# Seven of eight query tiles on float16 parts, and weight readings queued behind the modulation transfers

## The chip, the cores and the metric

The kernel runs on one core of one Trainium2 chip. The metric is the device time of one execution in microseconds; the median of three runs is given, and one more execution was recorded by the hardware profiler. The engines are TensorE (PE, with PEld for its weight loads), VectorE (DVE), ScalarE (ACT), GpSimd (POOL) and SyncE (SP). SP and POOL issue most of the DMA transfers, each strictly in its own order. An instruction waits on its engine until its inputs are there and its output buffer is free, and everything behind it on that engine waits too.

## The reference

Two blocks of a diffusion transformer over 256 tokens `x` and 256 context tokens `ctx`, width 2048, all in float32. Layer 0 mixes by a Fourier transform, layer 1 is windowed attention with context keys. Each layer is modulated by a shift, a scale and a gate, which are products of `silu(c)` with `ada_w`.

```python
shift, scale, gate = split(silu(c) @ ada_w[i] + ada_b[i])      # the same for the context
h = rmsnorm(x, norm_g[i]) * (1 + scale) + shift
# layer 0
u, z = split(h @ fnet_w_in)                                    # 2048 -> 4096 + 4096
f = real(fft2(u by groups of 256)) ; f = f @ w_mix             # 16 groups
x = x + gate * ((f * silu(z)) @ w_out[0])                      # 4096 -> 2048
# layer 1
q, k, v, z = split(h @ attn_w_in)                              # q: 64 heads of 64, k and v: 8 heads
o = softmax(rope(q) rope(k)^T / 8 with window, context and sink) v
x = x + gate * ((o * silu(z)) @ w_out[1])
return rmsnorm(x, final_g)
```

## The kernel before, in words

The kernel keeps float32 accuracy by splitting each operand in a high and a low part and multiplying three times (`mm3`: high·high, high·low, low·high; lines L145 to L147). There are two kinds of parts. `half_split` makes float32r parts `wh`, `wl`: a cast on ScalarE (L66) and a subtraction on VectorE (L67). `split16` makes float16 parts in one tile `wf`: a scaled copy on ScalarE (L137) and a scaled subtraction on VectorE (L138). Float16 needs a scale per weight matrix, a power of two that is found from the sum of the squares of the whole matrix. So a weight that is to be split in float16 has to be read once ahead of time, which is called a reading here: POOL loads half a weight tile (512 KB of float32) as a bfloat16 tile `sn` of 256 KB (`scan_load`, L821), and ScalarE squares it and sums (`scan_sums`, L836).

The stages in order of time, with their approximate place in the span:

- 0 to 370 us: modulation of layer 0, Fourier part.
- 370 to 658 us, the z stage: 28 blocks `b` of 48 matmuls each (`ps<-act,wf`), each with one 1 MB weight tile `raw` (SP), `y` (256 KB, SP), and readings.
- 658 to 1003 us, the output projection of layer 0: 32 steps `i` of 48 matmuls (`ps<-y,wf`), two halves of the output (`sw`) of 16 steps (`kg`) each. A step has one `raw` tile of 1 MB, split in two halves `wf` (for `kg` 14 and 15 in float32r parts). The second half's first step needs a scale that is made on VectorE as the first half ends (L843 and around).
- 1003 to 1112 us: sums, keys and values of layer 1.
- 1112 to 1565 us: attention. Eight query tiles (`wq`), 32 z tiles and 32 attention blocks, interleaved: per query tile four z tiles and four blocks.
- to the end: output projection of layer 1.

Beside the z stage and the first projection run 64 modulation jobs (`ada_jobs`): each loads two 512 KB pieces of `ada_w`, `zr` on SP and `wa` on POOL, and VectorE multiplies and sums them with L792 (twice a piece, in the last third of the jobs once). A step of the projection takes one job, in steps 6 to 9 and 17 to 25 two, in steps 14 to 16 and from 28 on none (`ada_rate`). `cb` (1 MB) is loaded four times for the jobs. `wa` tiles lie in the pool `ws` (six buffers) together with the split weights; `sn` tiles in the pool `act` (33 buffers).

The order of instructions on each engine is set by a scheduler that runs the program on a model of the chip. `tc.issue_after(x)` gives it an order to keep on the engine of `x`: what is traced inside comes after `x` there. It makes no new wait between engines.

Layer 1 multiplies query tiles 0 to 3 from the float32r parts `hx1` (in the profile `ps<-wh,h` and `ps<-wl,h`) and tiles 4 to 7 from the float16 parts `hz` (`ps<-wf,hzx`). Their scale `upq` comes from 32 readings of the weights of tiles 4 to 7, all made in the z stage (`scan_loadsq`). In the projection, readings are made of the rest of `wo0` (`scan_loads`, steps 0 to 13) and of `wkv` and `wo1b` (`scan_loads1`, by `w_rate`: 1 or 2 in steps 10, 11, 14 to 18 and 20, 2 in step 22, 3 in steps 24 and 26 to 28).

Of the kernel before, what the change touches and what calls it, by code (L numbers as in the profile page):

```python
# [32 lines left out]
def tile_dit(ctx: ExitStack, tc: tile.TileContext, a: dict, out: bass.AP):  # L33
    nc = tc.nc
# [20 lines left out]
    def act(dt=F32):  # L55
        return actp.tile([P, 512], dt, tag="act", name="act")
# [12 lines left out]
    def half_split(t, i):  # L69
        h = wsp.tile([P, 1024], F32R, tag="ws", name="wh")  # L70
        l = wsp.tile([P, 1024], F32R, tag="ws", name="wl")
        split(h, l, t[:, i * 1024 : (i + 1) * 1024])
        return h, l
# [695 lines left out]
    def ada_jobs():  # L769
        for pieces in ((0,), (1, 2, 3)):  # L770
            for kh in range(2):
                cb = adap.tile([P, 2, 1024], F32, tag="cb", name="cb")
                with tc.issue_after(hs_end[2]):
                    nc.gpsimd.dma_start(cb, a["crow"][:, kh].broadcast_to([P, 2, 1024]))
                with tc.issue_after(hs_end[1]):
                    S.activation(cb, cb, AF.Silu)
                order = [(i, fg) for i in pieces for fg in range(8)]
                if kh == 1 and len(pieces) == 3:
                    thirds = [(3, fg) for fg in range(8)]
                    order = order[:4] + [o for pair in zip(order[4:12], thirds) for o in pair] + order[12:16]  # L780
                if True:
                    for i, fg in order:
                        for f in range(2):
                            q = slice(f * 1024, f * 1024 + 1024)
                            if f == 0:
                                wf = adat.tile([P, 1024], F32, tag="zr", name="zr", bufs=2)
                                nc.sync.dma_start(wf, a["adw"][i, kh, fg][:, q])
                            else:
                                wf = wsp.tile([P, 1024], F32, tag="ws", name="wa")
                                nc.gpsimd.dma_start(wf, a["adw"][i, kh, fg][:, q])  # L790
                            for s in range(2 if i < 3 else 1):
                                V.tensor_tensor_reduce(junk if s == 0 and i < 3 else wf, wf, cb[:, s], 1.0, 0.0, ALU.mult, ALU.add, acc[:, i, kh, fg * 2 + f, s : s + 1])  # L792
                        if kh == 1 and fg == 7:
                            ada_done(i)
                        yield
        while True:
            yield

    out0 = [False]
    ada = ada_jobs()  # L800


# [9 lines left out]
    yq = adab[:, 1, 0].rearrange("p k s -> p (k s)")  # L812
    wst = [a["wkv"][i] for i in range(8)] + [a["wo1b"][i] for i in range(12)] + [a["wo1c"][i] for i in range(6)]
    scans1 = iter(range(52))
    scansq = iter(range(32))
    qsn = c32.rearrange("p k c -> p (k c)")[:, 0:32]

    def scan_load(src, j, col):
        t = actp.tile([P, 1024], BF16, tag="act", name="sn")
        c = j % 2 * 1024  # L820
        nc.gpsimd.dma_start(t, src[:, c : c + 1024])  # L821
        pend.append((t, col))

    def scan_loadsq(n):
        for j in [next(scansq) for _ in range(n)]:
            scan_load(a["wq"][4 + j // 8, j // 2 % 4], j, qsn[:, j : j + 1])

    def scan_loads1(n):
        for j in [next(scans1) for _ in range(n)]:
            c = j + 64  # L830
            scan_load(wst[j // 2], j, scn[:, c : c + 1])
# [29 lines left out]
    with tc.tile_pool(name="yp", reuse_waits="tile", bufs=32) as ypool:  # L861
# [174 lines left out]
        for i in range(32):  # L1036
# [7 lines left out]
            if i < 14:  # L1044
                scan_loads({6: 1, 7: 1, 8: 1, 9: 1}.get(i, 2))
            scan_loads1(w_rate.get(i, 0))
            if i == 14:
                osc.append(half_scale(1, half_sum(1)))
            if kg == 14:
# [96 lines left out]
    with tc.tile_pool(name="h1", reuse_waits="tile", bufs=16) as h1p:  # L1146
# [136 lines left out]
        with tc.tile_pool(name="at", reuse_waits="tile", bufs=2) as at:  # L1283
# [88 lines left out]
            def finish_q(hk, oq):  # L1372
                sq = at.tile([P, 2, 4], F32, tag="sq", name="sq")
                for tb in range(2):
                    S.activation(act(), oq[tb], AF.Square, scale=dnq if hk >= 4 else 1.0, accum_out=sq[:, tb, 0:1])
                x, up, sc = (sq[:, :, c] for c in (1, 2, 3))
                qr = [act(), act()]
                tab = ropeq if hk >= 4 else rope
                roped(qr[0], oq[0], 0, actp, "act", tab=tab)
                V.tensor_scalar(x, sq[:, :, 0], 2.0**-70, None, op0=ALU.max)  # L1380
                V.tensor_scalar(x.bitcast(I32), x.bitcast(I32), 24, 23, op0=ALU.logical_shift_right, op1=ALU.logical_shift_left)
# [48 lines left out]
            def prep(u):  # L1430
                kind, n, i, _ = u
                if kind == "o":
                    return w1_next()
                src = (kind, n, i // 2)
                if src not in raws1:
                    raws1[src] = raw(a["wq"][n, i // 2] if kind == "q" else a["wz1"][n])
                return split16(raws1[src], i % 2, upq) if kind == "q" and n >= 4 else half_split(raws1[src], i % 2)

            ready = {}
            pe_last = [None]  # L1440
# [1 line left out]
            def emit_unit():  # L1442
# [17 lines left out]
                if kind == "q":  # L1460
# [5 lines left out]
                    for j in range(2):  # L1466
                        k = i * 2 + j
                        q = slice(j * 512, (j + 1) * 512)
                        for tb in range(2):
                            t = hz[k][0] if n >= 4 else hx1[k]  # L1470
                            pe_last[0] = mm3(o[tb], t[:, tb * P : (tb + 1) * P], t[:, N + tb * P : N + (tb + 1) * P], wh[:, q], wl[:, q], k == 0, k == KT - 1)
                    if i == 7:
                        finish_q(n, o)
# [367 lines left out]
```

## Time and profile before

| | us |
|---|---|
| median of three runs (lowest, highest) | 1754.69 (1754.27, 1757.89) |
| the profiled execution | 1755.04 |
| its span, first to last instruction | 1753.3 |
| TensorE busy in it | 1702.5 (97%) |
| VectorE busy | 1376.5 (79%) |
| ScalarE busy | 1125.1 (64%) |
| mean granted TensorE clock | 0.992 of full speed |

Busy time of matmuls overlaps itself, since they are pipelined: a float16 matmul of 512 columns is shown with 379 ns but a new one starts every 215 ns. So stalls of PE are read here from the number of matmuls in a stretch. In the table of transfers a reading is counted with the 256 KB that it writes, though it reads 512 KB.

### The profile page before, as it was taken

What the parts mean: (1) busy time and instruction counts of PE and PEld (TensorE: products, weight loads), DVE (VectorE), ACT (ScalarE), POOL (GpSimd) and SP (SyncE); (2) the same over time, 40 slices, a digit from 0 to 9 for tenths busy, and PEclk for the clock granted to TensorE, in tenths of its full rate; (3) what the DMA queues carried; (4) which work ended last, traced back from release to release, by engine and by line L of the source; (5) the groups of instructions that cost most, each with busy time, mean ns of one, the idle gap of its engine ahead of it and who ended that gap; (6) DMA issues with size and microseconds to landing.
All of it is one profiled execution on the core that took longest, in us unless ns stands there. A gap on an engine that the chain in (4) does not pass through costs nothing. (4 is left out here: it accounts for less than half of the span.)

```text
span 1753.3 us, 28081 instructions
## 1 busy us (share of the span) xinstructions
PE 1702.5 (97%) x10379; PEld 1095.3 (62%) x10379; DVE 1376.5 (79%) x2395; ACT 1125.1 (64%) x1997; POOL 248.2 (14%) x372
## 2 busy tenths in 40 slices
PE   6999999999999999799979999999999999999997
PEld 4679999644444444345434564678887667876464
DVE  5779889798676884785679578688999999987755
ACT  5545556477887875363414379668878878887643
POOL 0002111211211113101210112200000000051002
PEclk9999999999999999899989999999999999999999
DMA  9998999789998989786888569269989999988643
GB/s 394 418 355 253 275 271 264 294 254 301 305 307 259 321 280 255 255 305 218 241 273 308 168 240 354 91 191 257 232 224 233 240 252 245 214 225 298 224 169 120
DMA packets 252393, 455.04 MB, mean 260 GB/s; under 512 B 170480, under 2 KB 170880, under 8 KB 225376
## 3 DMA queue, kind: packets, MB, share of 16 engines
q1 hardware_dynamic: 197568, 335.60, 59.2%
q0 software_dynamic: 50544, 110.70, 24.9%
q10 hardware_dynamic: 4144, 6.95, 1.1%
q8 instruction: 81, 1.33, 0.3%
q14 instruction: 56, 0.46, 0.1%
HBM read 436.14 MB, written 12.59 MB: 256 GB/s over the span
## 5 line engine op out<-in xcount | busy, mean ns | idle before, releaser
L146 PE MATMUL ps<-act,wf 128*128 128x512 f16 x512 | 194.0, 379 | 0.0
L147 PE MATMUL ps<-act,wf 128*128 128x512 f16 x512 | 191.1, 379 | 0.0
L67 DVE TENSOR_TENSOR wl<-raw,wh 128x1024 fp32r<-128x1024 f32 x120 | 150.8, 1266 | 50.9 <-ACT wh L66 29.1
L145 PE MATMUL ps<-act,wf 128*128 128x512 f16 x512 | 189.8, 379 | 0.6 <-ACT wf L137 0.5
L145 PE MATMUL ps<-y,wf 128*128 128x512 f16 x448 | 172.6, 386 | 10.2 <-ACT wf L137 10.2
L147 PE MATMUL ps<-y,wf 128*128 128x512 f16 x448 | 170.3, 384 | 9.6 <-DVE wf L138 9.6
L146 PE MATMUL ps<-y,wf 128*128 128x512 f16 x448 | 172.9, 386 | 0.0
L147 PEld LDWEIGHTS <-wf 128*128 128x128 f16 x960 | 94.3, 98 | 125.3 <-DVE wf L138 11.0
L145 PEld LDWEIGHTS <-wf 128*128 128x128 f16 x960 | 94.3, 98 | 124.7 <-ACT wf L137 14.2
L146 PEld LDWEIGHTS <-wf 128*128 128x128 f16 x960 | 94.6, 98 | 111.1 <-issue 3.8
L66 ACT CAST wh<-raw 128x1024 fp32r<-128x1024 f32 x120 | 124.3, 1045 | 59.2 <-PE ps L146 33.5
L137 ACT ACTIVATE wf<-raw,nrm 128x1024 f16<-128x1024 f32 x56 | 62.9, 1142 | 130.4 <-DVE acc L792 103.3
L145 PE MATMUL ps<-h,wh 128*128 128x256 f32 x512 | 144.8, 283 | 0.0
L146 PE MATMUL ps<-h,wh 128*128 128x256 f32 x512 | 142.2, 278 | 0.0
L147 PE MATMUL ps<-h,wl 128*128 128x256 f32 x512 | 142.2, 278 | 0.0
L138 DVE SCALAR_TENSOR_TENSOR wf<-raw,adab,wf 128x1024 f16<-128x1024 f32 x82 | 112.2, 1380 | 30.3 <-ACT wf L137 30.2
L836 ACT ACTIVATE sn<-sn 128x1024 bf16<-128x1024 bf16 x121 | 126.3, 1044 | 11.7 <-DMA sn<-in_wq 6.9
L1520 ACT ACTIVATE p<-ps,mx 128x512 f32<-128x512 f32 x128 | 87.9, 687 | 61.3 <-DVE mx L1516 61.3
L137 ACT ACTIVATE wf<-raw,adab 128x1024 f16<-128x1024 f32 x82 | 91.9, 1142 | 40.4 <-PE ps L147 16.3
L138 DVE SCALAR_TENSOR_TENSOR wf<-raw,tn,wf 128x1024 f16<-128x1024 f32 x64 | 79.9, 1282 | 46.4 <-ACT wf L137 46.3
L145 PEld LDWEIGHTS ps<-h,wh 128*128 128x128 f32 x512 | 96.1, 188 | 7.4 <-issue 5.1
L792 DVE CUSTOM_DVE_ANT_0 junk<-wa,cb 128x1024 f32<-128x1024 f32 x48 | 58.6, 1221 | 51.2 <-DMA wa<-in_adw 51.0
(444 smaller groups left out, 4691.5 us busy)
## 6 DMA issues: line engine op xcount, KB each, us to landing
raw<-in_wz SPq DMA_DIRECT2D x64, 1024.0 KB, 6.9
raw<-in_awp SPq DMA_DIRECT2D x32, 1024.0 KB, 12.7
zr<-in_adw SPq DMA_DIRECT2D x64, 512.0 KB, 7.0
wa<-in_adw POOLq DMA_DIRECT2D x64, 512.0 KB, 6.8
raw<-in_wo SPq DMA_DIRECT2D x32, 1024.0 KB, 7.6
raw<-in_wq SPq DMA_DIRECT2D x32, 1024.0 KB, 5.7
raw<-in_wu SPq DMA_DIRECT2D x32, 1016.0 KB, 6.5
sn<-in_wo POOLq DMA_DIRECT2D x64, 256.0 KB, 9.9
```

The costliest lines, as they stand in the source:

```text
L66: last_cast[0] = S.copy(h, src).ins
L67: last_sub[0] = eng.tensor_tensor(l, src, h.bitcast(F32), op=ALU.subtract).ins
L137: last_cast[0] = S.activation(w[:, 0], src, AF.Copy, scale=up).ins
L138: last_sub[0] = V.scalar_tensor_tensor(w[:, 1], src, up, w[:, 0], op0=ALU.mult, op1=ALU.subtract).ins
L145: PE.matmul(o, wh, xh, start=start, stop=False)
L146: PE.matmul(o, wh, xl, start=False, stop=False)
L147: return PE.matmul(o, wl, xh, start=False, stop=stop).ins
L792: V.tensor_tensor_reduce(junk if s == 0 and i < 3 else wf, wf, cb[:, s], 1.0, 0.0, ALU.mult, ALU.add, acc[:, i, kh, fg * 2 + f, s : s + 1])
L836: S.activation(t, t, AF.Square, accum_out=c)
L1520: S.activation(pt[hh, tb], so[hh, tb], AF.Exp, bias=mx[:, hh, tb : tb + 1], scale=-1.0, accum_out=sm[:, hh, tb : tb + 1])
```

## The change

Three things are done together.

1. Query tiles 1 to 3 also use float16 parts: `n >= 4` and `hk >= 4` become `>= 1` wherever a tile's parts, its rope table or the scale of its squares are chosen.
2. Their weights have to be read ahead too: 56 readings of `wq` where there were 32, beginning with tile 1. The z stage issues its 32 as before, and the other 24 come in the projection: one in each of the steps 4, 5, 10 to 13 and 17 to 25, three in each of the steps 14 to 16.
3. Every reading's transfer is tied behind the last `wa` transfer and the last cast that stand before it in the program.

```diff
@@ ada_jobs
-                                nc.gpsimd.dma_start(wf, a["adw"][i, kh, fg][:, q])
+                                last_wa[0] = nc.gpsimd.dma_start(wf, a["adw"][i, kh, fg][:, q]).ins
@@
-    scansq = iter(range(32))
-    qsn = c32.rearrange("p k c -> p (k c)")[:, 0:32]
+    scansq = iter(range(56))
+    qsn = c32.rearrange("p k c -> p (k c)")[:, 0:56]
 
     def scan_load(src, j, col):
         t = actp.tile([P, 1024], BF16, tag="act", name="sn")
         c = j % 2 * 1024
-        nc.gpsimd.dma_start(t, src[:, c : c + 1024])
+        with tc.issue_after(last_wa[0]) if last_wa[0] else nullcontext(), tc.issue_after(last_cast[0]):
+            nc.gpsimd.dma_start(t, src[:, c : c + 1024])
         pend.append((t, col))
 
     def scan_loadsq(n):
         for j in [next(scansq) for _ in range(n)]:
-            scan_load(a["wq"][4 + j // 8, j // 2 % 4], j, qsn[:, j : j + 1])
+            scan_load(a["wq"][1 + j // 8, j // 2 % 4], j, qsn[:, j : j + 1])
@@ the steps of the projection
             scan_loads1(w_rate.get(i, 0))
+            scan_loadsq(3 if i in (14, 15, 16) else i in (4, 5, *range(10, 14), *range(17, 26)))
@@ finish_q
-                    S.activation(act(), oq[tb], AF.Square, scale=dnq if hk >= 4 else 1.0, accum_out=sq[:, tb, 0:1])
+                    S.activation(act(), oq[tb], AF.Square, scale=dnq if hk >= 1 else 1.0, accum_out=sq[:, tb, 0:1])
-                tab = ropeq if hk >= 4 else rope
+                tab = ropeq if hk >= 1 else rope
@@ prep
-                return split16(raws1[src], i % 2, upq) if kind == "q" and n >= 4 else half_split(raws1[src], i % 2)
+                return split16(raws1[src], i % 2, upq) if kind == "q" and n >= 1 else half_split(raws1[src], i % 2)
@@ emit_unit
-                            t = hz[k][0] if n >= 4 else hx1[k]
+                            t = hz[k][0] if n >= 1 else hx1[k]
```

What this does to the order is seen best on POOL, whose queue holds both kinds of transfers. The first place is the turn from the z stage to the projection; `wa` is a modulation piece, `sn` a reading, `in_wq`, `in_wo`, `in_wkv` and `in_wo1b` the weights that are read. Before:

```order
L790 DMA wa<-in_adw 128x1024
L821 DMA sn<-in_wq 128x1024 x2
L821 DMA sn<-in_wo 128x1024 x18
L821 DMA sn<-in_wkv 128x1024
L790 DMA wa<-in_adw 128x1024
L821 DMA sn<-in_wo 128x1024 x2
L821 DMA sn<-in_wkv 128x1024
```

and after the change, at the same place (L821 is L823 there):

```order
L790 DMA wa<-in_adw 128x1024
L823 DMA sn<-in_wq 128x1024 x2
L823 DMA sn<-in_wo 128x1024 x6
L790 DMA wa<-in_adw 128x1024
L823 DMA sn<-in_wo 128x1024 x2
L790 DMA wa<-in_adw 128x1024
L823 DMA sn<-in_wo 128x1024 x2
L823 DMA sn<-in_wq 128x1024
L790 DMA wa<-in_adw 128x1024
```

Thirteen readings have moved from ahead of the second `wa` to behind it and behind later ones. The second place is POOL again, around step 17 of the projection, where two jobs a step begin (`xT` are pieces of x for the residual). Before:

```order
L1066 DMA act<-in_xT 128x512 x2
L790 DMA wa<-in_adw 128x1024 x2
L821 DMA sn<-in_wkv 128x1024 x10
L821 DMA sn<-in_wo1b 128x1024 x9
L790 DMA wa<-in_adw 128x1024 x18
```

and after:

```order
L1069 DMA act<-in_xT 128x512 x2
L823 DMA sn<-in_wkv 128x1024 x2
L823 DMA sn<-in_wq 128x1024 x3
L823 DMA sn<-in_wkv 128x1024
L823 DMA sn<-in_wq 128x1024
L790 DMA wa<-in_adw 128x1024 x2
L823 DMA sn<-in_wkv 128x1024
L823 DMA sn<-in_wq 128x1024
L790 DMA wa<-in_adw 128x1024 x2
L823 DMA sn<-in_wq 128x1024
L790 DMA wa<-in_adw 128x1024 x2
```

The nineteen readings in one piece now alternate with pairs of `wa`. The third place is ScalarE at steps 16 to 18, where the second half of the projection begins. `wf` are the splits of a step, `sn` the squares of readings (of `wkv` into `scn`, of `wq` into `c_98`), `act` the squares of finished outputs. Before:

```order
L836 ACTIVATE sn,scn<-sn 128x1024 x2
L992 ACTIVATE act<-act 128x512 x6
L137 ACTIVATE wf<-raw,nrm 128x1024 x2
L836 ACTIVATE sn,scn<-sn 128x1024 x2
L137 ACTIVATE wf<-raw,nrm 128x1024
L992 ACTIVATE act<-act 128x512
L137 ACTIVATE wf<-raw,nrm 128x1024
```

and after:

```order
L838 ACTIVATE sn,c_98<-sn 128x1024 x3
L994 ACTIVATE act<-act 128x512 x6
L137 ACTIVATE wf<-raw,nrm 128x1024 x2
L838 ACTIVATE sn,scn<-sn 128x1024 x2
L838 ACTIVATE sn,c_98<-sn 128x1024
L994 ACTIVATE act<-act 128x512
L838 ACTIVATE sn,c_98<-sn 128x1024 x2
L137 ACTIVATE wf<-raw,nrm 128x1024
L994 ACTIVATE act<-act 128x512
L137 ACTIVATE wf<-raw,nrm 128x1024
L838 ACTIVATE sn,scn<-sn 128x1024 x2
L838 ACTIVATE sn,c_98<-sn 128x1024 x3
```

Five squares stand between the splits of step 16 and those of step 17 where two stood, and five again before step 18.

1 line of the change is left out of this document (added).

## The prediction

> **What bounds the kernel now.** I read the page first (engine shares), then stretches of 25 us, then what the matrix engine waited for where it was short of work, and from there back through VectorE's and POOL's rows in time.
>
> ```profile
> PE 1702.5 (97%) x10379; PEld 1095.3 (62%) x10379; DVE 1376.5 (79%) x2395; ACT 1125.1 (64%) x1997; POOL 248.2 (14%) x372
> ```
>
> PE carries the span, so a change pays only where it shortens PE's own work or PE's idle time. The next table (one row per stretch) shows where the idle time lies:
>
> ```profile
> core 0: us, PE busy (x) PEld busy (x) DVE busy (x) ACT busy (x) POOL busy (x), PEclk, DMA share, GB/s
> 25.00:50.00 25.00, 24.01 (x204) 16.53 (x196) 13.63 (x43) 13.62 (x28) 0.00 (x0) 1.00 1.01 417
> 400.00:425.00 25.00, 25.00 (x121) 11.40 (x120) 20.36 (x38) 20.75 (x38) 4.13 (x8) 1.00 1.05 330
> ...
> 675.00:700.00 25.00, 25.00 (x118) 11.29 (x117) 8.88 (x11) 14.32 (x22) 7.53 (x15) 1.00 1.09 271
> 700.00:725.00 25.00, 21.42 (x87) 9.02 (x86) 16.65 (x26) 9.98 (x15) 3.21 (x6) 0.87 0.88 259
> 725.00:750.00 25.00, 19.25 (x76) 7.94 (x75) 21.82 (x35) 7.17 (x9) 2.65 (x5) 0.86 0.75 260
> 850.00:875.00 25.00, 25.00 (x117) 11.33 (x116) 14.48 (x21) 7.71 (x10) 3.72 (x7) 1.00 1.06 321
> 875.00:900.00 25.00, 15.62 (x66) 6.60 (x64) 11.33 (x17) 2.19 (x2) 5.04 (x10) 0.80 0.86 222
> ...
> 925.00:950.00 25.00, 25.00 (x118) 11.30 (x117) 24.98 (x39) 7.76 (x11) 2.65 (x5) 1.00 0.90 306
> ```
>
> A full stretch of layer 0's output projection runs about 116 matmuls (those at an edge count in two rows), 0.2155 us each, so one of its 32 steps of 48 matmuls takes 10.35 us. Three stretches fall short: 87, 76 and 66. That is 29 + 40 + 50 = 119 matmuls, or 26 us, missing; the lower granted clock (0.80 to 0.87) is inside this number. PE's waits of 690 to 760 and of 860 to 910 name what ended them:
>
> ```profile
> PE ps L147 <- DVE wf L138: 9.3, 2, 5.8
> ...
> PE ps L145 <- ACT wf L137: 9.4, 1, 9.4
> ```
>
> PE waited for split weights, and these stood in line behind VectorE's sums over the modulation weights:
>
> ```profile
> 701.25 1.23 DVE L792 CUSTOM_DVE_ANT_0 junk<-wa,cb 128x1024 f32<-128x1024 f32 x1 [14.61 <-DMA wa<-in_adw]
> ...
> 716.74 1.23 DVE L792 CUSTOM_DVE_ANT_0 junk<-wa,cb 128x1024 f32<-128x1024 f32 x1 [7.09 <-DMA wa<-in_adw]
> ...
> 888.64 1.23 DVE L792 CUSTOM_DVE_ANT_0 junk<-wa,cb 128x1024 f32<-128x1024 f32 x1 [23.14 <-DMA wa<-in_adw]
> ```
> ```profile
> 891.17 2.19 ACT L137 ACTIVATE wf<-raw,nrm 128x1024 f16<-128x1024 f32 x2 [26.61 <-DVE acc L792]
> ```
>
> So VectorE stood for 14.6, 7.1 and 23.1 us on a `wa` transfer, and the `wa` was late because POOL, which issues in order, had readings (`sn`) ahead of it:
>
> ```profile
> 689.93 0.53 POOL L821 DMA_DIRECT2D sn<-in_wkv  x1 [3.14 <-DMA sn<-in_wo]
> 691.75 0.53 POOL L790 DMA_DIRECT2D wa<-in_adw  x1 [1.29 <-DMA sn<-in_wo]
> ...
> 877.86 0.53 POOL L821 DMA_DIRECT2D sn<-in_wo1b  x1 [0.78 <-DMA sn<-in_wo1b]
> 879.11 0.53 POOL L790 DMA_DIRECT2D wa<-in_adw  x1 [0.72 <-DMA sn<-in_wo1b]
> ```
>
> **Readings behind the modulation transfers (the tie).** In the quoted order 21 readings stand between one `wa` and the next in the first place and 19 in the second; in the new order 8 and 2. A transfer passes every 1.25 us (877.86 to 879.11), so 13 to 17 fewer ahead of it bring the `wa` some 16 to 21 us earlier, about what VectorE waited. I therefore take both stalls as gone: −26 us, bounds −26 and, if the second one (50 matmuls, 11 us) stays, −15. The tie to the last cast names an instruction of ScalarE while the readings are POOL's; the order of POOL alone shows no effect of it, and I cost it at nothing.
>
> **Query tiles 1 to 3 on float16 parts.** The trace has both kinds of tile. A group of one query tile with its four z tiles and four attention blocks, from the tile's first matmul to the next tile's, is in float32 parts and in float16 parts:
>
> ```profile
> 1253.20:1310.20 57.00, 57.00 (x434) 47.40 (x432) 50.54 (x92) 45.67 (x88) 1.93 (x2) 1.00 0.89 236
> ...
> 1365.00:1419.80 54.80, 54.80 (x435) 38.50 (x434) 51.08 (x93) 45.22 (x88) 2.50 (x3) 1.00 1.00 237
> ```
>
> With the same number of matmuls the float16 group takes 2.2 us less; three tiles give −6.6 us. The mean durations of the two matmuls bound it from below: 396 − 379 = 17 ns, times 96 matmuls, times 3, is 4.9 us.
>
> ```profile
> L146 PE MATMUL ps<-wl,h 128*128 128x512 f32 x128 | 50.7, 396 | 0.0
> ...
> L146 PE MATMUL ps<-wf,hzx 128*128 128x512 f16 x192 | 72.3, 379 | 0.0
> ```
>
> The splits of 24 weight halves become dearer, on ScalarE 1142 − 1045 ns and on VectorE 1380 − 1266 ns each, 2.3 and 2.7 us in all:
>
> ```profile
> L66 ACT CAST wh<-raw 128x1024 fp32r<-128x1024 f32 x120 | 124.3, 1045 | 59.2 <-PE ps L146 33.5 <-PE ps L147 20.2 <-issue 2.0
> L137 ACT ACTIVATE wf<-raw,adab 128x1024 f16<-128x1024 f32 x82 | 91.9, 1142 | 40.4 <-PE ps L147 16.3 <-PE ps L146 10.2 <-DMA raw<-in_wq 5.3
> ...
> L67 DVE TENSOR_TENSOR wl<-raw,wh 128x1024 fp32r<-128x1024 f32 x120 | 150.8, 1266 | 50.9 <-ACT wh L66 29.1 <-issue 13.3 <-PE ps L147 7.9
> L138 DVE SCALAR_TENSOR_TENSOR wf<-raw,adab,wf 128x1024 f16<-128x1024 f32 x82 | 112.2, 1380 | 30.3 <-ACT wf L137 30.2
> ```
>
> PE covers that: VectorE is at 51.1 of 54.8 us in the float16 group, which pays the same dearer splits. Without that cover the 2.7 us would stand against the 6.6.
>
> **24 more readings.** All fall in steps 4, 5, 10 to 13, 17 to 25 (one each) and 14 to 16 (three each). Each adds a square on ScalarE (1.044 + 0.187 us, 29.5 us in all), a POOL issue of 0.53 us and a read of 512 KB that lands as 256 KB:
>
> ```profile
> L836 ACT ACTIVATE sn<-sn 128x1024 bf16<-128x1024 bf16 x121 | 126.3, 1044 | 11.7 <-DMA sn<-in_wq 6.9 <-DMA sn<-in_wkv 2.5 <-DMA sn<-in_wo 2.1
> L836 ACT ACTIVATION_READ_ACCUMULATOR sn<-sn 128x1 f32 x121 | 22.7, 187 | 0.0
> ```
> ```profile
> zr<-in_adw SPq DMA_DIRECT2D x64, 512.0 KB, 7.0
> wa<-in_adw POOLq DMA_DIRECT2D x64, 512.0 KB, 6.8
> ...
> raw<-in_wo SPq DMA_DIRECT2D x32, 1024.0 KB, 7.6
> ...
> sn<-in_wq POOLq DMA_DIRECT2D x32, 256.0 KB, 10.7
> ```
>
> ScalarE, at 2 to 14 of 25 us in the stretches above, hides its share except at the turn to the second half. There the scale of step 16 is ready only as step 15 ends, and the splits of step 17 follow close:
>
> ```profile
> 844.36 1.14 ACT L137 ACTIVATE wf<-raw,nrm 128x1024 f16<-128x1024 f32 x1
> ...
> 845.52 1.28 DVE L138 SCALAR_TENSOR_TENSOR wf<-raw,nrm,wf 128x1024 f16<-128x1024 f32 x1 [1.14 <-ACT wf L137]
> ...
> 851.76 0.38 PE L145 MATMUL ps<-y,wf 128*128 128x512 f16 x1
> ```
>
> The half is ready at 846.8 and wanted at 851.8. Three more squares before it (3.1 to 3.7 us) leave a bit over 1 us; if their transfers are late, up to 3 us of stall: I keep 0 to 3.
>
> The larger doubt is transfers. By the code steps 10 to 25 now move 16 `raw` tiles of 1 MB, 22 pairs `zr`+`wa`, one `cb` (1 MB), 46 readings and 8 `xT` (256 KB): 67 MB in 16 × 10.35 = 166 us, 405 GB/s read. The trace reaches 417 in the opening (25 to 50 us), so it fits, barely. In steps 17 to 25 VectorE has no room either (24.98 of 25 us), so longer landings count there. Loaded (400 to 520 us) against unloaded (895 to 965 us):
>
> ```profile
> zr<-in_adw SPq DMA_DIRECT2D x11, 512.0 KB, 7.5
> ...
> zr<-in_adw SPq DMA_DIRECT2D x13, 512.0 KB, 6.4
> ```
>
> At 1.1 us for each of 9 steps that is at most 10 us; at least nothing, if the lead that VectorE has at step 17 covers it. With the turn: 0 to 13 us. I take 6, the middle, since the new order leaves VectorE with the lead that the old one lost at 865.
>
> The Trainium skill speaks against the change here: its page "DMA: Bandwidth & Descriptors", section "Where 436 GB/s comes from", says that for transfers between HBM and SBUF the HBM side, about 358 GB/s per core, binds. By that figure the estimate for steps 10 to 25 would be 187 us, 22 us more than PE needs, and the time 1744. The trace does not agree, at 417 GB/s in a stretch bound by loading.
>
> **Sum.** The profiled execution took 1755.0 us (span 1753.3; 0.3 above the runs' median of 1754.7). 1755.0 − 26 − 6.6 + 6 = 1728.
>
> **The rivals.**
> 1. No new stall: the lead covers the transfers. 1755.0 − 32.6 = 1722. For it: in the z stage three readings a block, 3.9 MB in 10.35 us (380 GB/s), leave PE at 25.00 of 25 (400 to 425 us). Against it: 405 is more, and VectorE was at 20 there.
> 2. Steps 10 to 25 run at the transfers' pace. If 380 GB/s is all they get, 67 MB need 177 us, +11; at the z stage's mean (3.6 MB a block, 351 GB/s) 191, +25. Middle +18: 1740. For it: shares of 1.05 to 1.09 wherever readings are dense. Against: PE lost nothing at 1.09 (675 to 700).
> 3. One stall remains, since the `wa` of step 17 now stands behind 17 readings and inherits the second wait: +11 on rival 1, 1733; with new delays 1739.
> 4. Slower: ScalarE holds each next split until the last reading has landed, in steps 10 to 25. It decides where such a step takes over 12.4 us: 16 × 2.04 eats the 32.6. At 13 us a step: 1755 − 32.6 + 42 = 1765. For it: squares and splits share one in-order engine. Against: ScalarE idled only 11.7 us before 121 squares.
> 5. The float16 tiles give nothing, VectorE setting the pace: 1735. The two groups above speak against it.
>
> **How the numbers follow.** The forecast (1722 to 1735, its own range) 0.50; rival 1 0.17; rival 2 0.13; rival 3 0.07; rival 4 0.05; rival 5 0.05; something near no change 0.03. The range that holds 8 in 10 goes from 1720 to 1743, from rival 1 with a little more than counted up to rival 2. A measurement here tells about 0.2% (3.5 us) from no change: faster 0.90, same 0.04, slower 0.06.
>
> **What would show it.** Right: between 660 and 1000 us full stretches of 116 matmuls, the idle time before `junk<-wa` well under 51 us, no row with `wa` behind nine `sn`, all seven float16 groups near 54.8 us. Wrong: PE waits in steps 16 to 25 of over 13 us in sum, released by ScalarE's splits after `sn` landings or by VectorE after `zr`; groups still at 57 us; a DMA share pinned above 1.05 while PE is short of matmuls.

## The result and the profile after

The changed kernel took 1745.66 us (median of five, 1739.17 to 1745.99) beside 1754.27 us for the kernel before: ratio 0.9936, 95% interval 0.9917 to 0.9956. It is faster, by 8.6 us where I forecast 27, and 2.7 us above my range. Its profiled execution was the shortest of the five, 1739.17 us with a span of 1737.4. A later repeat gave 1739.92 beside 1758.04, ratio 0.9891 (0.9872 to 0.9911). The nine executions together lie between 1735.3 and 1746.5, so the repeat's median and the profiled execution lie inside my range and the first median outside it; that spread is taken up below.

The page's line of engine times, and stretches of 25 us that answer to those of before (stretch, width, PE, PEld, DVE, ACT, POOL, granted clock, DMA share, GB/s written):

```profile
PE 1694.0 (98%) x10379; PEld 1070.3 (62%) x10379; DVE 1381.1 (79%) x2395; ACT 1152.6 (66%) x2045; POOL 258.5 (15%) x396
```
```profile
700.00:725.00 25.00, 25.00 (x118) 11.35 (x116) 19.34 (x29) 10.92 (x16) 3.60 (x7) 1.00 0.87 269
725.00:750.00 25.00, 25.00 (x118) 11.32 (x116) 21.38 (x30) 8.90 (x12) 5.46 (x11) 1.00 0.93 303
...
800.00:825.00 25.00, 19.43 (x81) 14.60 (x80) 12.92 (x20) 13.42 (x24) 10.03 (x19) 0.93 1.05 291
875.00:900.00 25.00, 25.00 (x117) 11.35 (x116) 23.20 (x37) 11.80 (x17) 4.25 (x8) 1.00 1.04 363
925.00:950.00 25.00, 25.00 (x118) 11.37 (x116) 24.81 (x38) 13.03 (x19) 6.37 (x12) 1.00 1.03 308
1125.00:1150.00 25.00, 18.38 (x91) 8.03 (x91) 18.20 (x32) 13.86 (x23) 0.00 (x0) 0.80 0.52 159
```

The three short stretches of before are full (118, 118 and 117 matmuls). Two others are short: at 800 us, with 81 matmuls where two kernels below that have no stall there run 113 (32 × 0.2155 = 6.9 us), and at 1125 us. PE's waits in 790 to 820 us, then in 1120 to 1140 us, name the release:

```profile
PE ps L147 <- DVE wl L67: 5.6, 1, 5.6
```
```profile
PE ps L1407 <- ACT fq L1397: 5.9, 1, 5.9
```

The first is at the turn of steps 13 and 14, where the float32 halves `wl` begin. The second is at the transposes of q0 (query tile 0), the first thing in layer 1 that PE needs from finished query data (`fq`, the finished query tile after its rope, in two float16 parts).

The groups of query tiles, first two of before (q1, which the prediction didn't show, then one of the q2 and q3 kind), then q1, q2, q3 and q4 of after:

```profile
1139.40:1196.10 56.70, 55.76 (x402) 45.89 (x401) 51.56 (x96) 41.63 (x78) 4.29 (x2) 1.00 0.75 207
1196.10:1253.20 57.10, 57.10 (x434) 47.55 (x433) 51.45 (x97) 45.15 (x91) 2.69 (x3) 1.00 0.96 233
```
```profile
1119.40:1181.80 62.40, 55.78 (x401) 37.79 (x400) 54.38 (x97) 43.96 (x79) 3.52 (x3) 0.92 0.72 183
1181.80:1238.10 56.30, 55.48 (x434) 38.80 (x432) 50.19 (x92) 44.77 (x88) 1.13 (x1) 1.00 0.95 238
1238.10:1293.30 55.20, 55.20 (x434) 38.90 (x433) 51.66 (x95) 45.21 (x89) 2.80 (x3) 1.00 0.98 238
1293.30:1348.70 55.40, 55.24 (x434) 38.73 (x432) 51.58 (x95) 45.19 (x89) 2.42 (x2) 1.00 0.96 241
```

This gives the account of the two profiled executions. q1 starts at 1139.4 before and at 1119.4 after: −20.0 us, all in layer 0. From there to the start of q7 it is 335.1 us before and 339.9 after (1459.3 − 1119.4): +4.8. The rest is 278.8 and 278.1: −0.7. Together −15.9, the difference of the spans.

### Where the two new stalls come from

The first begins 40 us earlier. These are POOL's, ScalarE's and VectorE's rows around the second job group's `cb` (start, length, idle time before it and its release), of before and then of after:

```profile
770.03 0.53 POOL L774 DMA_DIRECT2D cb<-in_crow  x1 [9.61 <-DVE acc L792]
...
775.85 1.91 ACT L776 ACTIVATE cb<-cb 128x2048 f32<-128x2048 f32 x1 [3.86 <-DMA cb<-in_crow]
...
777.79 1.23 DVE L792 CUSTOM_DVE_ANT_0 junk<-zr,cb 128x1024 f32<-128x1024 f32 x1 [3.14 <-ACT cb L776]
```
```profile
757.72 0.54 POOL L774 DMA_DIRECT2D cb<-in_crow  x1 [8.77 <-DVE wf L138]
...
768.76 1.91 ACT L776 ACTIVATE cb<-cb 128x2048 f32<-128x2048 f32 x1 [10.90 <-DMA cb<-in_crow]
...
770.70 1.23 DVE L792 CUSTOM_DVE_ANT_0 junk<-zr,cb 128x1024 f32<-128x1024 f32 x1 [10.85 <-ACT cb L776]
```

From issue to the silu `cb` takes 5.8 us before and 11.0 after, and VectorE stands 10.85 us instead of 3.14. In the next steps it stands three times more for a late `wa`. All its waits for `cb`, `zr` and `wa` in 740 to 815 us add up to 10.7 us before and 20.0 after, and VectorE's lead over PE is gone at step 14.

The second stall, in VectorE's and ScalarE's rows at the end of q0, of before and then of after:

```profile
1136.76 3.62 DVE L67 TENSOR_TENSOR wl<-raw,wh 128x1024 fp32r<-128x1024 f32 x2 [0.34 <-ACT wh L66]
1140.30 0.68 DVE L1138 TENSOR_TENSOR act<-ps,rope 128x512 f32<-128x512 f32 x1
...
1146.63 1.34 ACT L1394 ACTIVATE fq<-act,sq 128x512 f16<-128x512 f32 x2 [0.66 <-DVE sq L1382]
```
```profile
1116.88 6.83 DVE L138 SCALAR_TENSOR_TENSOR wf<-raw,adab,wf 128x1024 f16<-128x1024 f32 x4 [0.42 <-ACT wf L137]
1123.64 0.68 DVE L1141 TENSOR_TENSOR act<-ps,rope 128x512 f32<-128x512 f32 x1
...
1129.89 2.47 DVE L138 SCALAR_TENSOR_TENSOR wf<-raw,adab,wf 128x1024 f16<-128x1024 f32 x2
1132.29 0.16 DVE L1385 TENSOR_SCALAR sq<-sq 128x2 int32<-128x2 int32 x1
...
1132.48 1.33 ACT L1397 ACTIVATE fq<-act,sq 128x512 f16<-128x512 f32 x2 [2.15 <-DVE sq L1385]
```

q0's matmuls end at 1139.1 before and 1119.1 after, so its rope starts 1.2 us later before and 4.5 us later after: four float16 subtractions of q1 stand ahead of it, and four more (two of them at 1129.89) stand between its rows. `fq` follows q0's end by 7.5 us before and 13.4 after, while q1's 36 matmuls ahead of the transposes take only 8.0 us. The split buffers seem to let it happen: a float32r half takes two of the six `ws` buffers (`wh`, `wl`), a float16 half one (`wf`), and ahead of q0's rope there now stand four of q1's splits where two stood. This is read from the code and the rows; no kernel with another number of buffers was run.

### The profile page after: what moved, and what is told of

It is laid out like the page before. It is cut to its first block, busy times and chain, and to the rows that moved or that the text cites. A ratio compares the mean times of both kernels' runs of the same rounds, so it can differ in the third digit from the quotient of the medians.

```text
span 1737.4 us, 28148 instructions
## 1 busy us (share of the span) xinstructions
PE 1694.0 (98%) x10379; PEld 1070.3 (62%) x10379; DVE 1381.1 (79%) x2395; ACT 1152.6 (66%) x2045; POOL 258.5 (15%) x396
## 5 line engine op out<-in xcount | busy, mean ns | idle before, releaser
L147 PE MATMUL ps<-act,wf 128*128 128x512 f16 x512 | 191.1, 379 | 0.0
L145 PE MATMUL ps<-act,wf 128*128 128x512 f16 x512 | 189.8, 379 | 0.6 <-ACT wf L137 0.2
L138 DVE SCALAR_TENSOR_TENSOR wf<-raw,adab,wf 128x1024 f16<-128x1024 f32 x106 | 144.9, 1379 | 37.6 <-ACT wf L137 37.6
L145 PE MATMUL ps<-y,wf 128*128 128x512 f16 x448 | 169.3, 379 | 0.8 <-ACT wf L137 0.8
L146 PE MATMUL ps<-y,wf 128*128 128x512 f16 x448 | 169.8, 379 | 0.0
L147 PE MATMUL ps<-y,wf 128*128 128x512 f16 x448 | 167.3, 379 | 0.0
L147 PEld LDWEIGHTS <-wf 128*128 128x128 f16 x960 | 93.8, 98 | 113.3
L145 PEld LDWEIGHTS <-wf 128*128 128x128 f16 x960 | 93.7, 98 | 113.3 <-ACT wf L137 4.2
L838 ACT ACTIVATE sn<-sn 128x1024 bf16<-128x1024 bf16 x145 | 151.3, 1044 | 12.8 <-DMA sn<-in_wq 8.3
L137 ACT ACTIVATE wf<-raw,adab 128x1024 f16<-128x1024 f32 x106 | 118.4, 1142 | 49.9 <-DMA raw<-in_wq 16.2
L67 DVE TENSOR_TENSOR wl<-raw,wh 128x1024 fp32r<-128x1024 f32 x96 | 120.8, 1263 | 33.1 <-ACT wh L66 16.8
L145 PE MATMUL ps<-h,wh 128*128 128x256 f32 x512 | 145.6, 284 | 0.1
L147 PE MATMUL ps<-h,wl 128*128 128x256 f32 x512 | 142.6, 279 | 0.9 <-DVE wl L67 0.9
L66 ACT CAST wh<-raw 128x1024 fp32r<-128x1024 f32 x96 | 99.1, 1042 | 52.2 <-PE ps L147 19.0
L146 PE MATMUL ps<-wf,hzx 128*128 128x512 f16 x288 | 108.9, 380 | 0.0
L145 PE MATMUL ps<-wf,hzx 128*128 128x512 f16 x288 | 108.6, 381 | 0.3 <-ACT hzx L1174 0.3
```

Source lines behind the costliest of these rows:

```text
L66: last_cast[0] = S.copy(h, src).ins
L67: last_sub[0] = eng.tensor_tensor(l, src, h.bitcast(F32), op=ALU.subtract).ins
L137: last_cast[0] = S.activation(w[:, 0], src, AF.Copy, scale=up).ins
L138: last_sub[0] = V.scalar_tensor_tensor(w[:, 1], src, up, w[:, 0], op0=ALU.mult, op1=ALU.subtract).ins
L145: PE.matmul(o, wh, xh, start=start, stop=False)
L146: PE.matmul(o, wh, xl, start=False, stop=False)
```

## The experiments

| kernel | median, us | ratio to before | 95% interval |
|---|---|---|---|
| tie_only | 1740.3 | 0.9916 | 0.9900 to 0.9931 |
| no_wa_tie | 1756.1 | 1.0000 | 0.9989 to 1.0010 |
| move4 | 1737.1 | 0.9892 | 0.9876 to 0.9908 |
| q1_late | 1742.2 | 0.9921 | 0.9908 to 0.9934 |
| after_again | 1739.9 | 0.9891 | 0.9872 to 0.9911 |
| q1_f32 | 1736.1 | 0.9881 | 0.9864 to 0.9899 |
| fix_b | 1753.5 | 0.9975 | 0.9964 to 0.9986 |
| fix_ab | 1748.2 | 0.9951 | 0.9933 to 0.9968 |
| q1_f32_move4 | 1733.5 | 0.9858 | 0.9841 to 0.9874 |
| late11_move4 | 1735.7 | 0.9872 | 0.9857 to 0.9887 |
| no_read | 1736.8 | 0.9876 | 0.9860 to 0.9893 |
| tiles_f32 | 1739.8 | 0.9898 | 0.9883 to 0.9913 |
| clear_q1f32 | 1726.4 | 0.9828 | 0.9804 to 0.9852 |
| clear_late11 | 1732.1 | 0.9856 | 0.9829 to 0.9884 |
| clear_four | 1729.8 | 0.9846 | 0.9819 to 0.9873 |
| clear_seven | 1735.7 | 0.9879 | 0.9859 to 0.9900 |

The kernel before, run beside them, had medians of 1755.2 to 1758.0 us.

### The tie alone, and everything but the tie

tie_only is the kernel before with this; no_wa_tie is the changed kernel without the first of the two ties:

```diff
+        with tc.issue_after(last_wa[0]) if last_wa[0] else nullcontext(), tc.issue_after(last_cast[0]):
             nc.gpsimd.dma_start(t, src[:, c : c + 1024])
```

> The kernel before with the tie alone: its 32 readings for q tiles 4 to 7 and its float32 q tiles 1 to 3 stay. Theory: the tie removes both stalls of steps 4 to 8 (26 us with what followed), and the new stall at 809 us of the changed kernel comes from the 24 added readings, which lengthen the landing of the second group's conditioning vector (cb, 11.0 us from issue to the silu, 5.8 before). Then 1754.3 - 26 = 1728, and PE runs through the turn of steps 13 and 14. Rival 1: that stall comes from the tied order itself, whatever the number of readings: 1728 + 6 = 1734, with the stall at the same turn. Rival 2: the tie gives nothing by itself: 1754.

> The changed kernel without the tie behind the modulation transfers; its 56 readings and seven float16 tiles stay. Theory: readings again stand ahead of modulation transfers on POOL's queue, the two stalls of steps 4 to 8 come back, and the readings added to steps 10 to 13 and 17 to 25 make at least as much again as they make in the changed kernel: 1746 + 20 = 1766 or more. Rival: the order on POOL was not the cause of the gain, and the time stays at 1740 to 1746.

Without the tie the gain is zero and both stalls of steps 4 to 8 are back (no_wa_tie, 700 to 750 and 875 to 900 us):

```profile
700.00:725.00 25.00, 19.90 (x86) 8.44 (x85) 14.32 (x21) 11.47 (x18) 6.92 (x13) 0.93 1.09 280
725.00:750.00 25.00, 19.44 (x81) 7.94 (x79) 22.11 (x34) 6.43 (x9) 2.64 (x5) 0.86 0.74 261
875.00:900.00 25.00, 20.41 (x89) 8.77 (x87) 11.39 (x16) 4.68 (x6) 6.35 (x12) 0.93 1.09 294
```

The 1766 expected for it was too high: the stall at 892 us shrank to half (89 matmuls in 875 to 900 us, where before had 66). The tie alone removes all three, and at the turn of steps 13 and 14 it loses nothing. The changed kernel differs from it by the added readings and the float16 tiles; tiles_f32 (below), with the readings and without the three tiles, has the stall, so the readings added by the change are needed for it. But it brings 16 us, not 26, because a stall that neither theory named opens at 927 us, 48 matmuls or 10 us (tie_only, 800 to 825 and 900 to 950 us):

```profile
800.00:825.00 25.00, 25.00 (x113) 18.69 (x112) 14.45 (x29) 8.14 (x14) 1.33 (x3) 1.00 0.70 230
...
900.00:925.00 25.00, 21.81 (x102) 9.67 (x99) 17.37 (x27) 5.74 (x8) 3.72 (x7) 1.00 0.86 282
925.00:950.00 25.00, 20.87 (x85) 8.79 (x86) 20.01 (x31) 9.77 (x14) 6.89 (x13) 0.86 0.83 239
```

In this kernel the scheduler put five of the six sums of a step's two jobs ahead of the step's first split on VectorE; in the changed kernel one or two. That this order makes the stall was not tried. The second tie, behind the casts, changes nothing: the changed kernel built without it is the same program.

### The stall at the turn of steps 13 and 14

move4 moves the four q readings of steps 10 to 13; the kernels called q1_f32_move4, late11_move4 and fix_ab have the same edit.

```diff
-            scan_loadsq(3 if i in (14, 15, 16) else i in (4, 5, *range(10, 14), *range(17, 26)))
+            scan_loadsq(3 if i in (14, 15, 16) else 2 if i in range(17, 21) else i in (4, 5, *range(21, 26)))
```

> The changed kernel with the four q readings of steps 10 to 13 moved to steps 17 to 20 (two there instead of one). Theory: the stall of 5.7 us at the turn of steps 13 and 14 comes from readings that share the transfers with the second group's cb and the wa behind it. Without them cb takes about 6 to 8 us to land instead of 11, the wait of VectorE for it shrinks by 3 to 5 us and the later waits for wa by some more, so the stall falls below 2 us: 1741 where the changed kernel gave 1745.7, 1735 where it gave 1739. Rival 1: cb lands late for another reason (its place on the queue, the 512-wide inputs): no change. Rival 2: the stall moves to steps 17 to 20, whose splits had 8 to 12 us of slack: no change in the time, a new stall there.

no_read leaves out all 15 readings of steps 9 to 13:

```diff
+        if no_read[0]:
+            V.memset(col, 1.0)
+            return
...
+            no_read[0] = i in range(9, 14)
```

> The changed kernel without the 15 readings of steps 9 to 13 (nine of layer 0's output weights, two of the next weights, four of q): these weights are missing from the sums that set the scales, and a constant stands in for each. Theory: the second group's cb lands late because readings share the transfers with it, those of the tie's new order (wo, wkv) as much as the added ones: without any, cb takes 6 us from issue to the silu instead of 11 and VectorE's waits in 740 to 815 us fall from 20 to 11 us or less, so no stall at the turn: 1738 where the changed kernel gave 1745.7, 1732 where it gave 1739. Rival: cb is slow because of the raw weights and zr on SP's queue, and takes 10 us or more without any reading; the stall stays at 3 us or more.

clear_q1f32 leaves nothing out and does the readings elsewhere (with q tile 1 in float32, next section, and the edit of move4):

```diff
-                scan_loads((2 if b % 3 else 1) if b < 28 else 0)
+                scan_loads(2 if b < 28 else 0)
-        w_rate = {10: 1, 11: 1, 14: 2, 15: 2, 16: 2, 17: 1, 18: 1, 20: 1, ...
+        w_rate = {14: 2, 15: 2, 16: 2, 17: 1, 18: 1, 19: 1, 20: 1, 21: 1, ...
-                scan_loads({6: 1, 7: 1, 8: 1, 9: 1}.get(i, 2))
+                scan_loads({6: 1, 7: 1, 8: 1, 9: 1}.get(i, 2) if i < 10 else 0)
```

> q tile 1 in float32, and no reading left in steps 10 to 13, all of them done elsewhere: the eight of layer 0's output weights in the z stage (two per block instead of one or two), the two of wkv in steps 19 and 21, the four of q in steps 17 to 20. Theory: readings that share the transfers with the second group's cb and the wa behind it are the whole cause of the stall at the turn of steps 13 and 14; with none there, cb takes 6 to 7 us, VectorE's waits in 740 to 815 us stay under 15 us and the stall under 2 us, where the same kernel with only the q readings moved still had 7.5: 1733.5 - 5.5 = 1728. Rival 1: the eight readings cost as much in the z stage, whose PE has no idle time but whose transfers are then 0.15 higher: a new stall there or in the first steps, 1733. Rival 2: the stall stays.

| | `cb`: issue to silu, us | last reading issued ahead of `cb` lands, us after `cb`'s issue | VectorE's waits for `cb`, `zr`, `wa`, 740 to 815 us | matmuls in 775 to 825 us |
|---|---|---|---|---|
| before | 5.8 | none in flight | 10.7 | 231 |
| tie_only | 10.0 | 5.2 | 13.3 | 229 |
| after | 11.0 | 8.5 | 20.0 | 197 |
| after_again | 11.1 | 8.5 | 23.4 | 181 |
| move4 | 10.6 | 7.1 | 17.2 | 224 |
| q1_f32_move4 | 12.3 | 9.2 | 18.7 | 195 |
| fix_ab | 11.9 | 7.6 | 18.4 | 206 |
| late11_move4 | 6.6 | 3.1 | 15.8 | 223 |
| no_read | 6.4 | none in flight | 14.5 | 221 |
| clear_q1f32 | 4.7 | none in flight | 7.0 | 229 |
| clear_seven | 5.1 | none in flight | 7.0 | 228 |

The loss goes with the waits: up to 13 us nothing is lost, at 14 to 17 some 5 to 8 matmuls, from 18 on 22 and more (228 to 232 are all; the traces not in the table agree). move4 lowered the time, but not by the step I named: `cb` stayed at 10.6 us, and VectorE's wait for it fell by 1.7 us, the waits for `wa` by 1.1. So it was no cure, and q1_f32_move4, with the same readings, lost as much as the changed kernel. With no reading around `cb` it takes 6.4 us (no_read), and with all of them moved away, 4.7. clear_seven (below), which differs from the changed kernel by the moved readings alone, has no stall there either. These are clear_q1f32's rows that answer to the ones of after:

```profile
758.04 0.53 POOL L774 DMA_DIRECT2D cb<-in_crow  x1 [9.47 <-DVE acc L792]
...
762.71 1.91 ACT L776 ACTIVATE cb<-cb 128x2048 f32<-128x2048 f32 x1 [2.31 <-DMA cb<-in_crow]
```
```profile
775.00:800.00 25.00, 25.00 (x117) 11.35 (x116) 23.05 (x34) 5.70 (x9) 8.03 (x15) 1.00 0.90 281
800.00:825.00 25.00, 25.00 (x113) 18.80 (x112) 9.52 (x20) 10.30 (x17) 5.78 (x11) 1.00 0.96 233
```

The readings are the cause, those of the tie's new order (`wo`, `wkv`) as much as the added ones: the tie alone already takes `cb` to 10.0 us, and the added readings lengthen the waits for `wa` behind it. The landings in the traces say which readings: in the eleven profiles where readings that POOL had issued ahead of `cb` were still in flight, `cb` landed 2.4 to 4.7 us behind the last of them; in the seven without such readings it landed 4.6 to 8.5 us after its own issue. Here are the last reading ahead, `cb`, and that reading's time from issue to landing, in move4 and then in late11_move4:

```profile
746.62 0.56 POOL L823 DMA_DIRECT2D sn<-in_wkv  x1
755.28 0.54 POOL L774 DMA_DIRECT2D cb<-in_crow  x1 [8.11 <-DVE acc L792]
...
sn<-in_wkv POOLq DMA_DIRECT2D x1, 256.0 KB, 15.7
```
```profile
747.79 0.56 POOL L823 DMA_DIRECT2D sn<-in_wkv  x1
759.09 0.54 POOL L774 DMA_DIRECT2D cb<-in_crow  x1 [10.74 <-DVE acc L792]
...
sn<-in_wkv POOLq DMA_DIRECT2D x1, 256.0 KB, 14.4
```

late11_move4 has move4's readings, but `cb` was issued 3.8 us later, when the last reading ahead needed 3.1 us more instead of 7.1, and took 6.6 us instead of 10.6, with three readings behind it in both. So the readings ahead count more than those behind. Why a reading itself takes up to 18 us to land there is not shown. clear_q1f32, at 1726.4 us (1725.1 to 1729.4), is the fastest of the study.

### The stall at q0's transposes

q1_late holds q1's splits back on VectorE, the fourth behind q0's rope, the later ones behind `fq`; q1_f32 leaves q1 in float32; fix_b holds the later ones behind the copy that follows the transposes (`turn_end`, L1408), and starts with 12 steps:

```diff
+                if (kind, n) == ("q", 1) and turn_end[0]:
+                    with tc.issue_after(turn_end[0]):
+                        return split16(raws1[src], i % 2, upq)
...
-                if pos[0] + 1 < len(ulist):
+                if pos[0] + 1 < len(ulist) and pos[0] != 11:
...
-            first = 11
+            first = 12
```

> The changed kernel with q tile 1's fourth split held on VectorE behind the rope of q tile 0, and its last four behind q0's two parts (fq). Theory: the new stall of 6.1 us at q0's transposes comes from VectorE, where four float16 subtractions of q1 (6.8 us) stand ahead of q0's rope and four more among it, because a float16 split takes one of the six split buffers where a float32 split took two. Held back, fq is ready some 3 to 5 us earlier and the stall falls to 1 to 3 us: 1741 where the changed kernel gave 1745.7, 1735 where it gave 1739. Rival: ScalarE's casts and squares, whose order stays nearly the same, set the time of fq: no change.

The rope now starts right after three splits, the transposes come 3.6 us earlier and the wait at the transposes is 2.4 us. But VectorE takes the four held splits before the copy of the transposes, and PE waits 3.0 us there (q1_late, VectorE's rows, then PE's wait):

```profile
1130.99 4.87 DVE L138 SCALAR_TENSOR_TENSOR wf<-raw,adab,wf 128x1024 f16<-128x1024 f32 x4
1135.78 0.68 DVE L1408 COPY qt<-ps 128x1024 f16<-128x1024 f16 x1
```
```profile
PE ps L1520 <- DVE qt L1408: 3.0, 1, 3.0
```

So the stall follows VectorE's place for the splits, as the theory says, but the gain I expected went into the next wait: q1 takes 63.0 us to q2. The rival (ScalarE sets it) falls, since ScalarE's order is nearly the same.

> The changed kernel with q tile 1 back on float32 halves (its readings still done): six float16 tiles of eight. Theory: the stall of 6.1 us at q0's transposes comes only from q1's float16 splits running ahead of q0's rope, so it falls below 1 us; q1 itself costs 2.2 us more on PE. From the start of q1 to the start of q7 335 to 336 us instead of 339.9: 1741 where the changed kernel gave 1745.7, 1735 where it gave 1739. Rival: the stall comes from the longer way to q0 (other order of layer 1's start) and stays, and the time goes up by 2 us.

This held: no wait above 0.4 us at the transposes, q1 56.7 us, q1 to q7 334.5 us.

> The changed kernel with q1's last four splits held on VectorE behind q0's transposes and the first of these also prepared later, and q1's fourth step on PE ahead of those transposes (12 steps first instead of 11). Theory: VectorE now goes from four splits to q0's rope, its parts and the copy with nothing of q1 in between, and PE has 2.7 us more to do meanwhile, so the two stalls of the former trial (2.3 at the transposes, 3.6 at the scores) fall together below 2 us: q1 takes 56 to 58 us to the start of q2 instead of 62.5, and the time is 1740 where the changed kernel gave 1745.7, 1734 where it gave 1739. Rival: VectorE has no room there (93% busy in every group), and the splits held back are missing later in the group: q1 stays at 61 us or more.

> Both trials that take away a new stall together: the four readings of steps 10 to 13 moved to steps 17 to 20, and q1's late splits behind q0's transposes. Theory: the two are independent, the first gave 1737.1, the second takes 5 to 6 us more: 1731 to 1732, which is 24 us below the kernel before. Rival: what the second gives is lost again in the later groups, whose splits come late: 1736 to 1737.

q1 fell to 56.1 us as expected, and yet both kernels are slower than the changed one. fix_b's q1, q2 and q4 (the prediction's columns):

```profile
1123.50:1179.60 56.10, 53.93 (x402) 37.18 (x402) 51.86 (x93) 42.11 (x76) 2.03 (x1) 1.00 0.77 197
1179.60:1240.20 60.60, 57.33 (x434) 40.39 (x432) 52.02 (x95) 44.76 (x88) 2.31 (x2) 0.97 0.91 236
...
1296.30:1353.80 57.50, 55.86 (x435) 39.08 (x434) 51.89 (x95) 44.96 (x89) 3.17 (x2) 1.00 0.96 226
```

Which part did it, the held splits or the twelfth step, late11_move4 tells: fix_ab's edit with `first = 11` (and `pos[0] != 10`).

> The moved readings, and q1's last five splits prepared behind q0's transposes as in the trial with 12 steps first, but with 11 steps first as in the changed kernel. Theory: the losses of that trial (q2 to q6 took 2 to 5 us longer each) came from the twelfth step, which moves every later step one place forward against the attention blocks that cover its splits, and not from the splits held back. With 11 steps q1 takes 57 to 59 us to the start of q2, q2 to q6 55 to 56 each, and the time is 1733. Rival: the splits held back are missing later, q2 takes 60 us again: 1745.

q1 took 58.8 us, q2 56.1, and the time was 1735.7 beside fix_ab's 1748.2. So the twelfth step was the fault: it moves every later step of q and z one place forward against the attention blocks, in all groups, and PE then waits at q2 to q6 for z's halves (`ps L147 <- DVE wl L67`, `ps L145 <- ACT wh L66`). My rival for fix_b (VectorE has no room) named the symptom, not the cause.

### The two together, and the worth of the float16 tiles

> q tile 1 on float32 halves and the four readings of steps 10 to 13 moved to steps 17 to 20: both new stalls of the changed kernel away, six float16 tiles left. Theory: the two are independent; q1 in float32 alone gave 1736.1 with a stall of 6.1 us (8.1 with the clock) left at the turn of steps 13 and 14, and moving the readings cut that to 1.4: 1730 to 1731. Rival: the two gains overlap or the stall of the turn varies from program to program (it was 3.5 us in the other kernel with moved readings): 1734 to 1736.

The rival came true (1733.5), for the reason in the table above. tiles_f32 puts tiles 1 to 3 back on float32 (`n >= 4` for `n >= 1` in the four places of the diff) and keeps all readings.

> The changed kernel with q tiles 1 to 3 back on float32 halves; all 56 readings are done. Theory: layer 0 is as in the changed kernel (a stall of 6 to 8 us at the turn of steps 13 and 14), and the three float16 tiles cost there what they should have brought: from the start of q1 to the start of q7 335 us instead of 339.9, so 1740 where the changed kernel gave 1745.7 and 1735 where it gave 1739; against the kernel with q1 alone in float32 (1736.1) 1 to 2 us more, which is then what float16 tiles 2 and 3 bring. Rival 1: the worth of 6.6 us that I forecast for the three tiles holds: 5 us slower than the changed kernel. Rival 2: no difference to the changed kernel.

q1 to q7 took 335.9 us, and the time was that of the changed kernel's repeat (1739.8 and 1739.9). So the three tiles bring nothing or less, and rival 1, my own price, falls. But its stall in layer 0 was longer than in q1_f32 (178 matmuls in 775 to 825 us), so single tiles are better compared where layer 0 has no stall. Four kernels, measured on two chips, have it so: four, six and seven float16 tiles, and seven with q1's splits held as in late11_move4.

> The same with all seven float16 tiles and q1's last splits held behind q0's transposes. Theory: layer 0 as in the other kernel of this pair, and q1 58.7 us to the start of q2 instead of 56.8, q2 to q6 the same: 1729 to 1731. The kernel with moved q readings and these held splits had no stall of over 2 us at the turn already, so its gain is the smaller: 1735.7 - 1 to 4. Rival: the first of the pair is faster by 2 us or more, and float16 in tile 1 is worth less than nothing even with the splits in the better order.

> No readings in steps 10 to 13, as in the kernel that gave 1726.4, but q tiles 1 to 3 in float32 (four float16 tiles, as in the kernel before): layer 0 has no stall, so the float16 tiles stand alone. Theory: tiles 2 and 3 together are worth 1 to 3 us, not the 4.4 forecast, since a float16 group here takes 55 to 56 us instead of 54.8: 1728 to 1729. Rival 1: the forecast price holds: 1731. Rival 2: they are worth nothing: 1726.

> The same layer 0 and all seven float16 tiles in the changed kernel's own order: the change as it was, with its readings moved out of steps 10 to 13 and nothing else. Theory: the stall of 6.1 us at q0's transposes is back and with it q1's 62.5 us; tile 1 in float16 costs 5 to 6 us: 1732. Rival: with layer 0 short, q1's splits no longer run ahead, and it gives 1727 to 1728.

They took 1729.8, 1726.4, 1735.7 and 1732.1 us (in the order four, six, seven, seven held). From the start of q1 to that of q7 it is 335.2, 333.3, 341.0 and 338.1 us. The first two groups (q1, q2) of clear_four, clear_q1f32 and clear_seven:

```profile
1112.20:1169.00 56.80, 55.86 (x402) 45.96 (x402) 51.66 (x96) 41.75 (x78) 4.31 (x2) 1.00 0.78 211
1169.00:1226.10 57.10, 57.10 (x434) 47.57 (x433) 51.21 (x97) 44.72 (x90) 2.69 (x3) 1.00 1.00 228
```
```profile
1114.10:1170.80 56.70, 55.76 (x402) 45.85 (x400) 51.46 (x96) 43.36 (x79) 2.30 (x2) 1.00 0.76 213
1170.80:1226.20 55.40, 55.03 (x435) 38.56 (x434) 51.21 (x93) 45.85 (x89) 2.90 (x2) 1.00 1.00 222
```
```profile
1112.30:1175.10 62.80, 56.19 (x401) 37.88 (x400) 54.36 (x97) 43.99 (x79) 3.52 (x3) 0.92 0.71 185
1175.10:1230.70 55.60, 55.03 (x434) 38.54 (x432) 50.01 (x92) 44.65 (x88) 1.14 (x1) 1.00 0.96 236
```

Tile 1 in float16 loses 9.3 us by the medians and 7.7 by the profile as the change has it, 5.7 and 4.8 with its splits held. Tiles 2 and 3 bring 1.9 us by the profile and 3.4 by the medians, whose intervals overlap: a gain that is likely, and smaller than the 4.4 forecast. The missing part is seen, not explained: with more float16 tiles the float16 groups q3 to q6 take 54.8 to 56.2 us here, where clear_four's three take 54.8 each.

### Why the same program took 1739 or 1746 us

> The changed kernel once more, beside the others on one chip. Its five times fell into two groups, 1739 to 1741 and 1746. Theory: the upper group is the same program with a longer stall at the turn of steps 13 and 14, where the second group's cb and wa land late by an amount that differs from run to run: a profile of the upper group would show 10 to 12 us there instead of 5.7 and the rest unchanged, and variants without that stall have a narrower spread. Rival: the spread is in the stages before 660 us or at the end, as in the kernel before, whose own runs spread by 4 to 6 us.

The profile this time was of the longest execution, 1746.46 us. Its stretch at the turn:

```profile
800.00:825.00 25.00, 17.66 (x68) 12.42 (x69) 13.99 (x21) 11.42 (x20) 9.54 (x18) 0.86 1.02 278
```

68 matmuls, where the short execution had 81. q1 starts at 1123.8 us, 4.4 later than in the short one; q1 to q7 takes 341.2 us, 1.3 more; the rest 1.6 more. So over half of the 7.3 us lies in the stretches ahead of q1, and most of that in this stall (16 matmuls in 775 to 825 us, 3.4 us). The theory holds for that part, and 2.9 us lie elsewhere. The spreads decide nothing: clear_q1f32, without the stall, spread by 4 us and the changed kernel by 11, but q1_late, with it, spread by 3, clear_four, without it, by 6, and the kernel before by up to 9. Two profiles are all that bears on it.

## Why the prediction was wrong, point by point

- **The tie, −26.** Right for the three short stretches: all are full, and without the tie the gain is gone (no_wa_tie). That the tie by itself gave 16 us, with another stall of 10, I had not foreseen.
- **New stalls, +6 (0 to 13).** The size was right by luck, since the place was wrong. Layer 0 became 20.0 us shorter in the profiled execution, exactly −26 + 6, but only 15.6 in the longest one. And the turn of steps 16 and 17 cost no more than before, and steps 17 to 25 (24.81 of 25 us on VectorE) nothing. What stalled was the turn of steps 13 and 14. I had `cb` in the sum of bytes and not as a step that VectorE, and behind it every job, waits for, and that lands behind the readings issued ahead of it.
- **Float16 tiles, −6.6.** This is the step that failed. It measured +4.8 us (q1 +5.7, q2 −0.8, q3 −1.8, q4 to q6 +1.7, with rounding). −6.6 to +4.8 is 11.4 us, and 1728 + 11.4 = 1739.4 is, but for 0.2 us, the profiled execution. The sign of being right that failed is "all seven float16 groups near 54.8 us": q1 took 62.4. The 2.2 us a tile came from groups between other float16 groups, and "PE covers that" from the middle of the attention stage. Tile 1 is not there: its splits stand beside q0's rope, with nothing for PE behind the 36 matmuls. I priced how long a split takes and not where it stands in VectorE's order; that a float16 half takes one buffer and not two is the likely reason why the splits ran ahead.
- **The median.** The remaining 6.5 us to 1745.7 are the spread between executions. Between the two profiled ones the stall at steps 13 and 14 makes 3.4 of 7.3 us; the rest is open. My range took in no such spread.
- **Rivals.** Rival 5 (the tiles give nothing) was nearest by its mechanism and had 0.05. Rival 2's 1740 was nearer by its number, but late transfers cost PE something in steps 10 to 13 only; from 850 to 950 us, at a share of 0.98 to 1.04, they left PE full. Rivals 1, 3 and 4 didn't happen.
- The Trainium skill's figure of 358 GB/s ("DMA: Bandwidth & Descriptors", "Where 436 GB/s comes from"), which gave 1744, names nearly the median, but the trace does not agree with its reason: 875 to 900 us shows 363 GB/s written, readings counted at half, with PE at 25.00 of 25.

The forecast time itself was reached by another program: with the readings out of steps 10 to 13 and q1 in float32, 1726.4 us.

## What to carry to other kernels

A transfer that a whole queue of work waits for needs a clear stretch ahead of it on its queue, even if the sum of bytes fits; look for the one-of-a-kind load (here `cb`, four times in the program) before the many. When a change makes an item take fewer buffers, ask how far ahead the engine will now run, and which instruction that another engine waits for gets pushed back. And a price measured in the middle of a stage doesn't hold for the piece at its edge.

## What the runs showed of the hardware that I had not expected

- One 1 MB load took 4.7 to 12.3 us from issue to use. With smaller loads of the same queue still in flight ahead of it, it landed 2.4 to 4.7 us behind the last of them (eleven profiles).
- The granted clock was below 1 in the stretches with a long stall (0.93 in that of 81 matmuls, 0.86 in that of 68, 0.80 at q0's transposes), and the matmuls lost exceed the wait: 6.9 us against 5.6 in the first.
- The same program, in the same stage, gave 68 or 81 matmuls in the same 25 us.
